# Gating an attention output before it is normalised, with one denominator product for two heads

## The chip, the cores and the metric

The kernel runs on one core of a Trainium2 chip. The metric is the device time of one execution in microseconds (us), as the median of several runs. Beside it stands a profile of one execution: which engine did what and when, what each instruction waited for, and the clock that TensorE (PE) was granted. The other engines are VectorE (DVE), ScalarE (ACT), GpSimd (POOL) and SyncE (SP), which here only issues DMAs.

## The reference

One inference step of a layer with three branches that read the same normalised input: dilated softmax attention (12 heads of 64 channels), a spatial gating unit and a gated linear recurrence. Every branch is gated by silu of its own projection, and one output projection joins them. There are 1024 prompt tokens and 8 single-token samples. What matters here is the prompt's attention. Each head evaluates three patterns of window and stride over the same keys, and combines them by their softmax denominators:

```python
PATTERNS = ((128, 1), (512, 4), (2048, 16))
...
    s = jnp.einsum('brnqhe,brnkhe->brnhqk', qb, kb, preferred_element_type=F32)
    s = jnp.where(valid[:, None], s, -jnp.inf)
    p, lse = _softmax_stats(s)
    o = jnp.einsum('brnhqk,brnkhe->brnqhe', p, vb.astype(F32))
...
    w = jax.nn.softmax(jnp.stack(lses), axis=0)
    return jnp.sum(w[..., None] * jnp.stack(outs), axis=0)
...
y = jnp.concatenate([o_a.reshape(B, L, C_A) * jax.nn.silu(z_a.astype(F32)), ...], axis=-1)
return x + jnp.einsum('bln,nd->bld', y, w_out)
```

Combined like this, the three patterns are one softmax in which each key is counted as often as patterns hold it. So for each head and query there is one sum of weighted values and one denominator: their quotient, times silu of the gate's projection, is what goes on to the output projection.

## The kernel before, in words

The attention (`attention`, line 514) goes through six pairs of heads, p = 0 to 5, two pairs to a step `sp`. For each pair `qk_proj` (287) projects queries and keys, and `qk_layout` (389) turns them so that channels lie on the partitions. For each step `v_proj` (333) projects the values of four heads, and `az_proj` (378) the gates: `Z` holds one tile `z` per pair, already silu of the projection, with the pair's two heads on partitions 0 to 63 and 64 to 127 and the tokens along the free dimension. Weights and inputs are split into a high and a low part (float32r), so that one product in full precision takes three passes of TensorE.

`attn_head` (423) does one head. First come, block by block, the products `s` of queries and keys, of which only the row maximum is kept (line 436, VectorE); the maxima go, as one more row, into the query operand. Then the head's queries are done in two halves `qc` of 512. A half goes through groups of products `st` (lines 470, 471); for each there is an exponential (473, ScalarE), a mask that also counts (476 to 485, VectorE), a cast to the high part `phi` (487, ScalarE) and the low part `plo` (488, VectorE). Lines 491 to 493 sum the weighted values in the PSUM tile `pv`: rows 0 to 63 are channels, and row 64, for which the value operand holds ones, is the denominator. In the second half one group (`parts is None`) takes every fourth key and query, so its operands are read in steps of four.

At the end of a half, before the change: ScalarE copies `pv` to SBUF as `yo` (498), and turns row 64 into its reciprocal by Ln and Exp (499, 500). TensorE spreads this one row over 64 partitions by a product with a column of ones, into `pb` (502). VectorE multiplies `yo` by `pb` into `rd`, writing the queries back in their natural order (503), and `z` by `rd` (505). After both heads SyncE stores `z` to DRAM (512), from where the output projection, the program's last stage, reads it.

The order of the work is not that of the text. The text gives each instruction its priority, and a scheduler (`TileContext` with a simulated timeline) builds each engine's queue from it, filling gaps with later work that is ready. Each engine then runs its queue strictly in order. Projections of the next pairs, and near the end those of the recurrence (`pi`, `pc`, `pcz`), so fill TensorE's gaps in the attention. What can run ahead is limited by buffers: PSUM has four tiles "st" (shared by `s`, `st` and `pb`), two for projections, one for transposes and one `pv`; SBUF has 16 large tiles (among them `z`, the projected queries and keys and the eight layout tiles of a pair) and two tiles "s2b" (`yo` and `rd`; later the recurrence's `kT` and others).

After the attention come the recurrence (`hgrn`, 744), with the samples' attention, the gating unit (`sgu`, 775) and the output projection (`out_proj`, 945). In the recurrence line 710 has a product `pn` of ones (128x128) with a tile of 512 columns.

`masks` (279) holds two masks in bf16; `cmask` has eight blocks of 128 columns, of which the last two are zero and are not read.

Of the kernel before, what the change touches and what calls it, by code (L numbers as in the profile page):

```python
# [8 lines left out]
F32 = mybir.dt.float32  # L9
# [3 lines left out]
AF = mybir.ActivationFunctionType  # L13
ALU = mybir.AluOpType
# [14 lines left out]
E = 64  # L29
# [62 lines left out]
def hybrid_step(tc, ins, outs, parts=("A", "D", "B", "C", "O"), dbg=None):  # L92
    nc = tc.nc
# [5 lines left out]
    def mm(out, lhsT, rhs, start, stop):  # L99
        nc.tensor.matmul(out, lhsT=lhsT, rhs=rhs, start=start, stop=stop)  # L100

    with tc.tile_pool(name="const", bufs=1) as cp, tc.tile_pool(name="sb", bufs=1) as sb, \
# [14 lines left out]
        def s2b(nm, dt=F32, shape=(P, 512)):  # L117
            return sb.tile(list(shape), dt, tag="s2b", name=nm, bufs=N_S2B)
# [7 lines left out]
        def psum(tag, nm, bufs, n=512):  # L126
            return pm.tile([P, n], F32, tag=tag, name=nm, bufs=bufs)
# [16 lines left out]
        def p_big(nm):  # L144
            return psum("st", nm, 4)
# [23 lines left out]
        ones = cp.tile([P, P], F32, name="ones")  # L169
# [36 lines left out]
        for t in (0, NT, *range(1, NT)):  # L206
            n = P if t < NT else NS
# [6 lines left out]
            if t == NT:  # L214
                nc.vector.tensor_tensor_reduce(out=xn[:n, :], in0=xt[:n, :], in1=xt[:n, :], op0=ALU.mult, op1=ALU.add,
                                               scale=1.0, scalar=0.0, accum_out=ss[:n, 0:1])
# [61 lines left out]
        new_k, new_v = (outs[n][0, 0].rearrange("s h e -> s (h e)") for n in ("o_kp", "o_vp"))  # L278
        masks = sb.tile([P, 2, NT, P], BF16, tag="mask", name="masks", bufs=1)
        cmask, nmask = (masks[:, i].rearrange("p a b -> p (a b)") for i in range(2))  # L280
        tc.keep_in_program_order(nc.gpsimd.dma_start(masks[:, 0], ins["cmask"]))
        tc.keep_in_program_order(nc.gpsimd.dma_start(masks[:, 1], ins["nmask"]))
        qkg = cp.tile([P, 2, 6], F32, name="qkg")
        tc.keep_in_program_order(nc.scalar.dma_start(qkg[:, 0, :], ins["q_norm_g"][0].rearrange("(a p) -> p a", p=P)))
# [138 lines left out]
        def attn_head(p, h, tiles, V, F, z):  # L423
# [3 lines left out]
            for qc in range(2):  # L427
                M = small(f"M{p}_{h}_{qc}", 12, tag="M")
                for b in range(4 * qc, 4 * qc + 4):
                    n = (b + 1) * P  # L430
# [16 lines left out]
            for qc in range(2):  # L447
                pv = p_pv(f"pv{p}_{h}_{qc}")
                pv4 = pv.rearrange("p (b r i) -> p b r i", b=4, r=4)
                groups = GROUPS[qc]  # L450
                for gi, parts in enumerate(groups):
# [4 lines left out]
                    if parts is None:  # L456
                        for r in range(4):
                            q4 = [x[:, 512:S].rearrange("p (b r i) -> p b r i", b=4, r=4)[:, :, r, :] for x in (QQ, Q1)]
                            prods.append((slice(r * P, (r + 1) * P), slice(r, 512, 4), q4, fh[:, r], fl[:, r],
                                          lambda m, r=r: pv4[0:m, :, r, :]))  # L460
# [17 lines left out]
                    elif parts[-1][0] == 3:  # L478
                        for c, m in ((0, P), (2 * P, 2 * P)):
                            n = 2 * P - c // 2  # L480
# [8 lines left out]
                    for i, (cols, _, _, v, l, out) in enumerate(prods):  # L489
# [3 lines left out]
                        mm(out(E + 1), v1, plo[:, cols], False, gi == len(groups) - 1 and i == len(prods) - 1)  # L493
                r = slice(h * E, (h + 1) * E)
                cs = slice(qc * 512, qc * 512 + 512)
                yo, rd = (s2b(f"{n}{p}_{h}_{qc}") for n in ("yo", "rd"))
                dr = yo[E:E + 1, :]
                nc.scalar.copy(yo[0:E, :], pv[0:E, :])
                nc.scalar.activation(dr, pv[E:E + 1, :], AF.Ln)  # L499
                nc.scalar.activation(dr, dr, AF.Exp, scale=-1.0)  # L500
                pb = p_big(f"pb{p}_{h}_{qc}")
                mm(pb[0:E, :], ones[E:E + 1, 0:E], dr, True, True)
                nc.vector.tensor_tensor(rd[r, :].rearrange("p (b i r) -> p b r i", b=4, r=4),
                                        *(x[0:E, :].rearrange("p (b r i) -> p b r i", b=4, r=4) for x in (yo, pb)), ALU.mult)
                nc.vector.tensor_tensor(z[r, cs], z[r, cs], rd[r, :], ALU.mult)

        def attn_core(p, nats, V, z, tiles=None):
            tiles = tiles or qk_layout(p, nats)
            F = v_far(p)
            for h in range(2):  # L510
                attn_head(p, h, tiles[h], V, F, z)
            nc.sync.dma_start(y_d[p * P:(p + 1) * P, :], z[:, :S])

        def attention():
            for sp in range(3):
                n0 = qk_proj(2 * sp, blk_first if sp == 0 else None)
                tiles = qk_layout(2 * sp, n0)
                V = v_proj(sp)
                Z = az_proj(sp)
                attn_core(2 * sp, n0, V[0], Z[0], tiles)  # L520
                n1 = qk_proj(2 * sp + 1)
                attn_core(2 * sp + 1, n1, V[1], Z[1])


        U32, U16 = mybir.dt.uint32, mybir.dt.uint16
# [504 lines left out]
        if "A" in parts:  # L1030
            attention()
# [30 lines left out]
```

## Time and profile before

| | us |
|---|---|
| median of 3 runs | 1364.37 (1363.49 to 1366.2) |
| the profiled execution | 1367.91 |
| its span, first to last instruction | 1366.1 |
| mean TensorE clock granted in it | 0.951 of full speed |

Reading it: a row of grouped instructions has line, engine, operation, output<-inputs, shapes and count, then the busy time and the mean of one in ns, then the idle time of the engine just before them and what ended it. The rows on one tile give the shortest, median and longest duration in ns instead. All matrix products have line 100 (a helper), so they are told apart by the names of their tiles. A row of a timeline has the start, the duration, and in brackets the idle time before and what ended it. A row of waits has who waited for whom, us in total, how often, and the longest. A row of windows has the stretch, its length, the busy time of each engine in it, and after these TensorE's clock, the busy share of the DMA engines and GB/s. A plain f32 product counts as two instructions, one for each pass; TensorE's matmuls overlap, so the step from one start to the next, not the duration, is what each takes.

### The profile page before, as it was taken

Reading aid. Unit: us, or ns where it says so; the run is one execution under the profiler, and the core shown is the slowest. Engines: PE = TensorE matmul, PEld = TensorE weight load, DVE = VectorE, ACT = ScalarE, POOL = GpSimd, SP = SyncE. Lnnn points to the kernel's source line nnn. Section 1 sums busy time; section 2 is a strip of 40 time slices with the busy share of each in tenths; the row PEclk is TensorE's granted clock in tenths of the full one; section 3 lists DMA queues with packets and bytes.
Section 4 is the critical chain, followed back from the end, with each engine's and each line's share of the span. In section 5 each row is a group of like instructions: output and inputs, shape, how many; then the busy total and the mean of one; then the engine's idle time right before and its main releaser. Section 6 shows DMA issues by size and latency. Waiting matters only on the chain. (4 is left out here: it accounts for less than half of the span.)

```text
span 1366.1 us, 27783 instructions
## 1 busy us (share of the span) xinstructions
PE 1277.9 (94%) x10634; PEld 1160.8 (85%) x10634; DVE 914.3 (67%) x2439; ACT 661.0 (48%) x1510; POOL 292.6 (21%) x267
## 2 busy tenths in 40 slices
PE   4799999999889999999999998998899999999999
PEld 3699798779779797898888888987788899899998
DVE  5835775565774656668888988888887623654653
ACT  4435454454443554456654744545544423544543
POOL 2531210131121212112202020211111135311221
PEclk9899899889999799999999999999999999999999
DMA  6241122220221212202433243434253313612210
GB/s 220 42 141 36 47 66 70 59 68 18 58 84 58 76 36 77 65 29 67 119 97 109 90 121 115 111 97 134 61 156 96 92 32 108 207 51 81 74 46 31
DMA packets 165044, 114.23 MB, mean 84 GB/s; under 512 B 13944, under 2 KB 158864, under 8 KB 164912
## 3 DMA queue, kind: packets, MB, share of 16 engines
q1 hardware_dynamic: 157520, 110.28, 27.3%
q10 hardware_dynamic: 6816, 1.54, 0.5%
q8 instruction: 83, 1.36, 0.4%
q0 software_dynamic: 576, 0.64, 0.3%
q14 instruction: 49, 0.40, 0.1%
HBM read 84.60 MB, written 22.09 MB: 78 GB/s over the span
## 5 line engine op out<-in xcount | busy, mean ns | idle before, releaser
L100 PE MATMUL pqk<-wh_qk,h 128*128 128x256 f32 x768 | 159.6, 299 | 5.2 <-ACT h L233 2.8
L100 PE MATMUL pc<-h,wh_cqf 128*128 128x344 f32 x576 | 144.1, 332 | 4.5 <-DVE cz L152 4.5
L100 PE MATMUL po<-woh,yl 128*128 128x256 f32 x512 | 145.0, 284 | 1.9 <-POOL yl L1011 1.9
L100 PE MATMUL po<-woh,yh 128*128 128x256 f32 x512 | 145.7, 285 | 0.0
L100 PE MATMUL po<-wol,yh 128*128 128x256 f32 x512 | 144.4, 282 | 0.0
L100 PEld LDWEIGHTS pqk<-wh_qk,h 128*128 128x128 f32 x768 | 131.5, 204 | 9.8 <-ACT h L233 3.0
L100 PE MATMUL pqk<-wl_qk,h 128*128 128x256 f32 x384 | 114.0, 297 | 0.0
L100 PEld LDWEIGHTS pc<-h,wh_cqf 128*128 128x128 f32 x576 | 102.1, 194 | 7.1 <-DVE cz L152 5.0
L100 PEld LDWEIGHTS po<-woh,yh 128*128 128x128 f32 x512 | 97.1, 190 | 5.6 <-ACT yh L1010 3.9
L100 PEld LDWEIGHTS po<-woh,yl 128*128 128x128 f32 x512 | 97.2, 190 | 4.1 <-POOL yl L1011 2.4
L100 PEld LDWEIGHTS po<-wol,yh 128*128 128x128 f32 x512 | 97.3, 190 | 0.0
L100 PE MATMUL pc<-h,wl_cqf 128*128 128x344 f32 x288 | 94.9, 332 | 2.5 <-POOL wl_cqf L193 2.2
L436 DVE CUSTOM_DVE_ANT_0 s<-s,masks 128x512 f32<-128x512 f32 (+2 forms) x144 | 77.7, 584 | 13.8 <-PE s L100 13.3
L100 PE MATMUL pi<-wh_ci,h 128*128 128x256 f32 x384 | 77.6, 297 | 4.8 <-DVE dsc L925 1.9
L100 PE MATMUL pv<-wh_v,h 128*128 128x256 f32 x384 | 79.1, 297 | 1.9 <-DVE ss L165 1.6
L473 ACT ACTIVATE st<-st 128x512 f32<-128x512 f32 (+2 forms) x84 | 44.2, 536 | 72.9 <-PE st L100 70.2
L100 PEld LDWEIGHTS pqk<-wl_qk,h 128*128 128x128 f32 x384 | 78.1, 204 | 0.5
L100 PE MATMUL pcz<-h,wh_cz 128*128 128x344 f32 x288 | 71.5, 326 | 0.3 <-DVE q L152 0.3
L100 PE MATMUL paz<-h,wh_az 128*128 128x344 f32 x288 | 71.1, 329 | 0.0
L100 PEld LDWEIGHTS pi<-wh_ci,h 128*128 128x128 f32 x384 | 64.2, 201 | 6.9 <-issue 2.9
L1011 DVE TENSOR_TENSOR yl<-yb,yh 128x512 fp32r<-128x512 f32 x44 | 30.4, 692 | 58.0 <-ACT yh L1010 58.0
L100 PEld LDWEIGHTS pv<-wh_v,h 128*128 128x128 f32 x384 | 65.7, 204 | 3.0 <-ACT yo L499 1.8
(376 smaller groups left out, 3665.1 us busy)
## 6 DMA issues: line engine op xcount, KB each, us to landing
wro<-in_w_out_dram SPq DMA_DIRECT2D x32, 256.0 KB
wr_qk<-in_w_in_dram SPq DMA_DIRECT2D x48, 128.0 KB
wr_cqf<-in_w_in_dram SPq DMA_DIRECT2D x48, 128.0 KB
dk<-in_cache_k_dram SPq DMA_DIRECT2D x24, 192.0 KB
dv<-in_cache_v_dram SPq DMA_DIRECT2D x24, 192.0 KB
xt<-in_x_prompt_dram SPq DMA_DIRECT2D x8, 512.0 KB
xr<-in_x_prompt_dram SPq DMA_DIRECT2D x32, 128.0 KB
out_o_yp_dram<-xr SPq DMA_DIRECT2D x32, 128.0 KB
```

What stands on the lines that cost most here:

```text
L100: nc.tensor.matmul(out, lhsT=lhsT, rhs=rhs, start=start, stop=stop)
L436: nc.vector.tensor_tensor_reduce(out=ps[:, :w], in0=ps[:, :w], in1=nmask[:, S - n + c:S - n + c + w], op0=ALU.add, op1=ALU.max, scale=1.0, ...
L473: nc.scalar.activation(st[:, :o], st[:, :o], AF.Exp)
L1011: (nc.gpsimd if piece == 0 else nc.vector).tensor_tensor(yl[:, sl, :], y, yh[:, sl, :].bitcast(F32), ALU.subtract)
```

## The change

The half no longer normalises. Row 64 of `pv` is copied into a row of a tile `den[qc]` (row 64 for the first head, row 96 for the second; the rest is zero), and `z` is multiplied by the channels of `pv` straight from PSUM, which also puts the queries in order. A new `normalise` does the rest, once for a pair and half: one product with a 128x128 tile `sel`, which holds ones at (64, 0 to 63) and (96, 64 to 127), puts both heads' denominators on all 128 partitions; Ln and Exp run on these in PSUM, and one multiplication of `z` by them ends it. It is called after the next pair's `qk_proj`, for the last pair at the end. `sel` lies in the two blocks of `cmask` that are not read, and the mask's load leaves these out; the two `den` are the two tiles "s2b". The store of `z` moves into `normalise`.

```diff
+        sel = masks[:, 0, 6:8].rearrange("p a b -> p (a b)").bitcast(F32)
+        tc.keep_in_program_order(nc.gpsimd.dma_start(masks[:, 0, 0:6], ins["cmask"][:, 0:6]))
-        tc.keep_in_program_order(nc.gpsimd.dma_start(masks[:, 0], ins["cmask"]))
...
-                yo, rd = (s2b(f"{n}{p}_{h}_{qc}") for n in ("yo", "rd"))
-                dr = yo[E:E + 1, :]
-                nc.scalar.copy(yo[0:E, :], pv[0:E, :])
-                nc.scalar.activation(dr, pv[E:E + 1, :], AF.Ln)
-                nc.scalar.activation(dr, dr, AF.Exp, scale=-1.0)
-                pb = p_big(f"pb{p}_{h}_{qc}")
-                mm(pb[0:E, :], ones[E:E + 1, 0:E], dr, True, True)
-                nc.vector.tensor_tensor(rd[r, :].rearrange("p (b i r) -> p b r i", b=4, r=4),
-                                        *(x[0:E, :].rearrange("p (b r i) -> p b r i", b=4, r=4) for x in (yo, pb)), ALU.mult)
-                nc.vector.tensor_tensor(z[r, cs], z[r, cs], rd[r, :], ALU.mult)
+                nc.scalar.copy(den[qc][E + 32 * h:E + 32 * h + 1, :], pv[E:E + 1, :])
+                zv = z[r, cs].rearrange("p (b i r) -> p b r i", b=4, r=4)
+                nc.vector.tensor_tensor(zv, zv, pv4[0:E], ALU.mult)
...
+        def normalise(p, z):
+            for qc in range(2):
+                cs = slice(qc * 512, qc * 512 + 512)
+                pb = p_big(f"pb{p}_{qc}")
+                mm(pb, sel, den[qc], True, True)
+                nc.scalar.activation(pb, pb, AF.Ln)
+                nc.scalar.activation(pb, pb, AF.Exp, scale=-1.0)
+                zv = z[:, cs].rearrange("p (b i r) -> p b r i", b=4, r=4)
+                nc.vector.tensor_tensor(zv, zv, pb.rearrange("p (b r i) -> p b r i", b=4, r=4), ALU.mult)
             nc.sync.dma_start(y_d[p * P:(p + 1) * P, :], z[:, :S])
+        den = [s2b(f"den{i}") for i in range(2)]
+        for t in (sel, *den):
+            nc.gpsimd.memset(t, 0.0)
+        for h in range(2):
+            nc.gpsimd.memset(sel[E + 32 * h:E + 32 * h + 1, h * E:(h + 1) * E], 1.0)
...
         def attention():
+            done = None
             for sp in range(3):
                 n0 = qk_proj(2 * sp, blk_first if sp == 0 else None)
+                if done:
+                    normalise(*done)
                 tiles = qk_layout(2 * sp, n0)
                 V = v_proj(sp)
                 Z = az_proj(sp)
-                attn_core(2 * sp, n0, V[0], Z[0], tiles)
+                done = attn_core(2 * sp, n0, V[0], Z[0], tiles)
                 n1 = qk_proj(2 * sp + 1)
-                attn_core(2 * sp + 1, n1, V[1], Z[1])
+                normalise(*done)
+                done = attn_core(2 * sp + 1, n1, V[1], Z[1])
+            normalise(*done)
```

More of the change, by code (lines that the diff above doesn't have):

```diff
@@ L511, in attn_core @@
                 attn_head(p, h, tiles[h], V, F, z)
-            nc.sync.dma_start(y_d[p * P:(p + 1) * P, :], z[:, :S])
+            return p, z
+        def normalise(p, z):
[7 more added lines that the diff above has]
+                nc.vector.tensor_tensor(zv, zv, pb.rearrange("p (b r i) -> p b r i", b=4, r=4), ALU.mult)
+            nc.sync.dma_start(y_d[p * P:(p + 1) * P, :], z[:, :S])
+        den = [s2b(f"den{i}") for i in range(2)]
[3 more added lines that the diff above has]
+            nc.gpsimd.memset(sel[E + 32 * h:E + 32 * h + 1, h * E:(h + 1) * E], 1.0)
         def attention():
+            done = None
             for sp in range(3):
                 n0 = qk_proj(2 * sp, blk_first if sp == 0 else None)
+                if done:
+                    normalise(*done)
                 tiles = qk_layout(2 * sp, n0)
```

## The prediction

> **What bounds the kernel now.** I read the page first, then the attention stage in the table of windows, the instructions of tile `yo`, TensorE's waits, the timeline around `pb`, and the clock in windows of 3.41 us.
>
> ```profile
> span 1366.1 us, 27783 instructions
> ...
> PE 1277.9 (94%) x10634; PEld 1160.8 (85%) x10634; DVE 914.3 (67%) x2439; ACT 661.0 (48%) x1510; POOL 292.6 (21%) x267
> ```
> ```profile
> 118.00:690.00 572.00, 542.06 (x3631) 478.56 (x3630) 382.80 (x941) 287.88 (x614) 108.65 (x109) 0.92 0.22 63
> ```
>
> TensorE (PE) bounds the program: 1277.9 of 1366.1 us busy. In the attention stage (118 to 690 us; columns: length, busy PE, PEld, DVE, ACT, POOL, granted clock, DMA) it is idle for 572 - 542.06 = 29.9 us, and a mean clock of 0.92 takes 572 × 0.08 = 46 us more. Three things pay here: less work on PE, fewer waits of PE, less time at the low clock.
>
> The change touches the end of each of the 24 half heads:
>
> ```profile
> L100 PE MATMUL pb<-yo,ones x48: 587/638/1111, 133.0 to 668.4; 1*64 1x512 f32 x48
> L498 ACT COPY yo<-pv x24: 566/580/583, 128.5 to 662.5; 64x512 f32<-64x512 f32 x24
> L499 ACT ACTIVATE yo<-pv x24: 588/590/592, 129.1 to 663.0; 1x512 f32<-1x512 f32 x24
> L500 ACT ACTIVATE yo<-yo x24: 608/627/629, 130.3 to 664.3; 1x512 f32<-1x512 f32 x24
> ```
> ```profile
> PE pb L100 <- ACT yo L500: 12.5, 5, 3.2
> ```
> ```profile
> 132.98 1.07 PE L100 MATMUL pb<-yo,ones 1*64 1x512 f32 x2
> 133.98 0.51 PE L100 MATMUL st<-QQ,KK 128*128 128x512 f32 x1
> ```
> ```profile
> 260.48 0.28 PE L100 MATMUL pv<-pl,vh 128*65 128x256 f32 x1
> 263.25 1.96 PE L100 MATMUL pb<-yo,ones 1*64 1x512 f32 x2 [2.49 <-ACT yo L500]
> 265.14 0.80 PE L100 MATMUL st<-QQ,KK 128*128 128x512 f32 x1
> ```
>
> After the last `pv` ScalarE copies and takes Ln and Exp (0.58 + 0.59 + 0.63 us); then PE spreads the one row, two passes in 1.00 us (132.98 to 133.98), and only behind it come the next `st`. Projections mostly fill the time; five times nothing was left, and PE stood still for 12.5 us in all, as at 260.76.
>
> The low clock comes in whole windows of 3.41 us on a fixed grid. First the seven windows that hold a `pb` of a head's first half and are full of work; then what follows each:
>
> ```profile
> 133.27:136.68 3.41, 3.41 (x15) 2.65 (x14) 2.36 (x3) 0.79 (x2) 0.61 (x1) 1.00 0.13 38
> ...
> sum 23.88, PE 23.88 PEld 17.77 DVE 15.28 ACT 9.30 POOL 3.64; mean PE 3.41 PEld 2.54 DVE 2.18 ACT 1.33 POOL 0.52
> ```
> ```profile
> 136.68:140.09 3.41, 3.41 (x17) 3.40 (x17) 2.59 (x4) 1.94 (x4) 0.00 (x0) 0.50 0.00 0
> ...
> sum 40.97, PE 40.36 PEld 37.86 DVE 31.10 ACT 23.25 POOL 1.27; mean PE 5.77 PEld 5.41 DVE 4.44 ACT 3.32 POOL 0.18
> ```
>
> PE had no idle time in any of the seven, and yet the clock then fell to 0.50 for one to three windows: 40.36 busy us at half speed, 20.2 us lost. After the five waits it fell too:
>
> ```profile
> 262.99:276.65 13.66, 12.87 (x52) 9.82 (x53) 9.01 (x14) 5.74 (x11) 0.00 (x0) 0.50 0.19 47
> ...
> sum 34.14, PE 33.10 PEld 26.59 DVE 27.55 ACT 17.50 POOL 11.71; mean PE 6.62 PEld 5.32 DVE 5.51 ACT 3.50 POOL 2.34
> ```
>
> That is 33.10 / 2 = 16.5 us. Behind every first-half `pb` stands the same block of `st`, whose loads are slow. Is it the block or the product that brings the clock down? Two windows tell:
>
> ```profile
> 176.70 1.07 PE L100 MATMUL pb<-yo,ones 1*64 1x512 f32 x2
> ```
> ```profile
> 177.65:181.06 3.41, 3.41 (x19) 3.32 (x19) 3.25 (x6) 1.99 (x6) 0.00 (x0) 1.00 0.31 71
> 181.06:184.48 3.42, 3.42 (x31) 3.42 (x30) 3.39 (x10) 2.96 (x6) 0.00 (x0) 1.00 0.02 5
> 904.69:908.11 3.42, 1.97 (x19) 1.07 (x21) 3.34 (x10) 0.86 (x2) 0.00 (x0) 1.00 0.25 79
> 908.11:911.52 3.41, 3.36 (x114) 3.04 (x114) 2.60 (x8) 3.35 (x8) 0.00 (x0) 1.00 0.28 82
> ```
> ```profile
> 906.54 1.12 PE L100 MATMUL pn<-csq,ones 128*128 128x512 f32 x2
> ```
>
> At 176.70 the grid puts `pb` into the window before (only 0.04 us falls into this one), the whole block into 177.65 to 181.06, and the clock stays at 1.00. So the block alone does not do it; a product with one row of weights seems to count as almost no work. The product `pn`, of the new product's shape (128 rows, 128 columns, 512 wide, f32), does count: its window is busy for only 1.97 us, over half of that with `pn`, and the clock holds.
>
> **The Trainium skill** ("TensorE: Matmul & The Clock Gate", Part 1) says the same of the window (free-running, about 3.4 us, half clock after an idle one), and the trace agrees. But its rule is about idle gaps: by that rule the seven full windows owe nothing to `pb`. That is rival B.
>
> **The change part by part.** The sum is made against the profiled execution: 1367.91 us, 1.8 outside its span, and 3.5 above the median of 1364.37.
>
> Work of PE. 24 products of one row go, 12 with 128 rows come. `pn` takes 1.12 us where `pb` takes 1.07, so each slot stays 1.0 to 1.05: -24.0 + 12.2 = **-11.8**.
>
> Waits of PE. The chain copy, Ln, Exp before a product becomes one copy of a row (0.58; the rows of L498 and L499 bound it at 0.57 and 0.59), and the product moves to the pair's end. Late next at 260.76 is the `st` block, which at 265.14 waits for nothing once `pb` is out. Of 12.5 I take two thirds, **-8**: the last third stays where the new product comes straight after the pair's last copy, because the projections that it stands behind were already used up as filling. Bounds: 0 and -12.5.
>
> Clock. Bounds: 0, and -20.2 - 16.5 = -36.7. I take three quarters of the seven full windows, **-15**, and nothing of the rest, since idle time from other causes can bring those down as well.
>
> ScalarE loses 24 × 1.80 = 43 us and gains 24 × 0.58 + 24 × 0.58 = 28 (Ln and Exp of 128x512, the row of L473 below). With 288 of 572 busy, this is worth nothing by itself.
>
> ```profile
> L193 POOL TENSOR_TENSOR wl_qk<-wr_qk,wh_qk 128x512 fp32r<-128x512 f32 x24 | 32.7, 1387 | 66.3 <-ACT wh_qk L192 64.9 <-DMA wr_qk<-in_w_in_dram 1.4
> ```
>
> POOL's five memsets (two of 128x512, the others smaller) run at the start, while POOL waits for ScalarE's casts (64.9 us of its idle time over the run end with one); uncovered they are shorter than two of L193, 2.8 us once. SyncE's six stores of `z` move behind the next pair's loads and `ko` stores; the loads queued behind a store then wait for the last multiplication, as they now wait for L505; what the stores write is read only in the last stage. `z` keeps its one of 16 buffers through the next projections; the next pair's eight layout tiles need the eight of this pair, which come free sooner. Were a layout to wait for `z` after all, that is the pair's end below once more, 6 × 2 = 12 us.
>
> VectorE:
>
> ```profile
> L503 DVE TENSOR_TENSOR rd<-yo,pb 64x512 f32<-64x512 f32 x24 | 25.8, 1077 | 48.2 <-PE pb L100 48.0
> L505 DVE TENSOR_TENSOR az<-az,rd 64x512 f32<-64x512 f32 x24 | 18.8, 785 | 0.6
> L488 DVE TENSOR_TENSOR pl<-st,ph 128x512 fp32r<-128x512 f32 x60 | 40.2, 684 | 2.5 <-ACT ph L487 1.7
> L414 DVE SCALAR_TENSOR_TENSOR Q<-tr,qkg,QQ 64x128 fp32r<-64x128 f32 x80 | 22.8, 347 | 15.2 <-ACT QQ L411 15.2
> L481 DVE SCALAR_TENSOR_TENSOR st<-st,masks 128x128 f32<-128x128 f32 x12 | 3.5, 292 | 0.1
> L485 DVE SCALAR_TENSOR_TENSOR st<-st,masks 128x512 f32<-128x512 f32 x48 | 32.7, 693 | 8.5 <-ACT st L473 8.1
> ```
> ```profile
> L473 ACT ACTIVATE st<-st 128x512 f32<-128x512 f32 x60 | 34.6, 582 | 62.6 <-PE st L100 60.1 <-DVE cz L152 2.0
> L487 ACT CAST ph<-st 128x512 fp32r<-128x512 f32 x60 | 34.0, 586 | 3.5 <-DVE st L485 3.1 <-DVE st L476 0.2
> ```
> ```profile
> ACT QQ L411 <- DVE Q L414: 11.3, 6, 4.1
> ```
>
> L503 writes every fourth element and takes 1.077; the contiguous L488 takes 0.684. The new multiplications both read and write `z` in that step. Bounds for one: 1.08 (reading costs nothing more) and 1.08 + 0.39 = 1.47 (it costs as much as writing). L414, which reads in this step, takes 0.055 more than L481 on 128 elements, 0.22 on 512: 1.30, my value. In all 36 × 1.30 = 46.8 for 24 × 1.862 = 44.7.
>
> The pair's end: behind its last `pv` VectorE now does three of these for one L503 and L505, 3.90 - 1.86 = 2.04 more, just where the next pair's `s` need it: 6 × 2.04 = 12.2, of which I put half on the path, **+6**.
>
> The handover of `pv`, of which there is one buffer: L411 waits for L414 in another half of the same PSUM tile, so I expect the multiplication to wait for the copy: 0.58 + 1.30 = 1.88 until `pv` is free, for 1.17 now, 0.71 later. Behind that wait stand the next half's masks on VectorE and its `pv` on PE. Cover: that `pv` needs exp, mask, cast and difference first (0.58 + 0.69 + 0.59 + 0.68 = 2.54). Without cover 24 × 0.71 = 17; I take a sixth, **+3**.
>
> Sum: -11.8 - 8 - 15 + 6 + 3 = -25.8: 1342.1 by the profiled execution, **1338.6** by the median. PE is busy for 94% of the whole span, so what follows the stage is bound by it too, and the gain should reach the end.
>
> **The rivals.**
>
> A, all the low windows go, and all the waits: -11.8 - 12.5 - 36.7 + 9 = -52, 1312. For it: after 262.99 the low clock lasted four windows, the block running at half speed. Against: of the 46 us, 0.5 × (40.97 + 34.14) = 37.6 stand behind a `pb` or its wait; 8 are low clock of another cause, so other gaps bring it on as well. Chance 0.12.
>
> B, the low clock is not the product's doing: -11.8 - 8 + 9 = -10.8, 1353.6. For it: the block is in all seven windows. Against: 177.65. Chance 0.14.
>
> C, "behind the projections" holds in name only, and reading in steps costs its full 0.39: then 3 × 1.47 - 1.86 = 2.55 at each pair's end, 15.3 in all, and 0.88 at each handover, half of it open, 10.6; with the waits gone and the clock as it is -11.8 - 12.5 + 25.9 = +1.6, 1366, no change. For it: L503's price for writing. Against: L414's. Chance 0.10. The Trainium skill ("SBUF — State Buffer", section "Door 1: The DMA port swizzle", the note on 16-byte cachelines) lets every access that goes to a new line pay, reads too; by that rule C's price is right; no run so far shows a multiplication that reads SBUF in this step.
>
> D, slower: VectorE holds the single `pv`. It is busy for 67% of the stage, so the multiplication may stand behind one more operation (0.69): 0.58 + 0.69 + 1.47 = 2.74 for 1.17, 1.6 us a half. If PE has nothing to put there, 24 × 1.6 = 38, and without a gain in clock -11.8 - 12.5 + 38 = +14: 1378. It decides from (11.8 + 12.5) / 24 = 1.0 us of idle PE a half on. For it: five times PE had nothing else. Against: the `st` block is now free to fill the gap. Chance 0.14.
>
> **How the numbers follow.** The forecast keeps 0.50 (its own range 1326 to 1352). About 0.2%, 2.7 us, is what a measurement can tell from no change. Faster: the forecast, A and B, 0.76; same: C, 0.10; slower: D, 0.14. The range 1310 to 1366 takes in all but D and some tails.
>
> **What would show it.** Right: 24 passes of the new product with 128 rows; PE's waits for it under 4 us; no window of 3.41 us that is full of work followed by clock 0.50; the stage's clock above 0.94; multiplications near 1.30. Wrong: `pv` waiting for VectorE's multiplication in PE's list, the clock still at 0.92, `s` waiting at each pair's start.

## The result, and the profile after

The changed kernel takes 1289.34 us (median of four runs, 1287.74 to 1294.63), the kernel before beside it 1363.93: a ratio of 0.9451, 95% interval 0.9429 to 0.9472. That is 74.6 us less, where 25.8 were forecast; the range, 1310 to 1366, ends above it. The profiled execution took 1287.74 us.

First the head of the page and, from the table of windows, the attention stage (before, this was 118 to 690 us; now it ends at about 585):

```profile
span 1286.0 us, 27698 instructions
...
PE 1215.2 (94%) x10610; PEld 1129.3 (88%) x10610; DVE 916.5 (71%) x2427; ACT 644.2 (50%) x1486; POOL 285.5 (22%) x272
```
```profile
118.00:585.00 467.00, 454.21 (x3330) 420.75 (x3329) 349.49 (x863) 253.28 (x551) 98.02 (x104) 0.98 0.25 71
```

TensorE is still the bound, but its clock in the stage is 0.98 instead of 0.92, and VectorE and ScalarE are busier in a shorter stage. The stage gave more than the whole program kept. The last store of `z` in SyncE's timeline, before and after:

```profile
672.49 0.35 SPq L512 DMA_DIRECT2D y_scr<-az  x1
```
```profile
572.99 0.34 SPq L517 DMA_DIRECT2D y_scr<-az  x1
```

99.5 us earlier, while the span is 80.1 shorter: the other 19.4 us are projections of the recurrence that had filled gaps in the attention and now run behind it (253 products `pc` start ahead of that store before, 144 after).

The groups of the new half's and pair's end, and TensorE's list of waits in the stage, from its top:

```profile
L499 DVE TENSOR_TENSOR az<-az,pv 64x512 f32<-64x512 f32 x24 | 26.1, 1088 | 13.5 <-ACT den L497 13.2
L497 ACT COPY den<-pv 1x512 f32<-1x512 f32 x24 | 13.9, 578 | 23.7 <-PE pv L100 23.5
L516 DVE TENSOR_TENSOR az<-az,pb 128x512 f32<-128x512 f32 x12 | 13.1, 1088 | 4.8 <-ACT pb L514 4.8
L100 PE MATMUL pb<-den,masks 128*128 128x512 f32 x24 | 12.3, 596 | 0.0
```
```profile
PE s L100 <- DMA QQ<-QQ: 6.9, 3, 2.4
PE pc L100 <- DVE cz L152: 2.7, 1, 2.7
PE pqk L100 <- DVE nat L304: 1.1, 2, 0.7
PE pv L100 <- DVE pl L489: 0.9, 1, 0.9
```

No wait for `pb` is left, and none of `pv` for the multiplication. The multiplications take 1.09 us. What low clock is left in the stage up to its last 3 us (four windows) stands behind idle time, as here:

```profile
179.70:183.10 3.40, 1.04 (x9) 0.84 (x7) 2.08 (x8) 1.22 (x2) 0.00 (x0) 1.00 0.17 39
183.10:189.90 6.80, 6.15 (x28) 5.43 (x27) 6.57 (x24) 2.26 (x5) 0.74 (x1) 0.50 0.33 77
```

Every profiled execution can be split in the same way, from the first lines of its page and its mean clock: idle time of PE is span less PE's busy time; what the low clock took is span × (1 - clock); the rest is PE's work at full clock. Before: idle 88.2, low clock 66.9, rest 1210.9. After: 70.8, 29.6, 1185.6. So of 80.1 us, **37.3 are clock, 25.3 work, 17.4 idle time**. (The clock has three digits, so its part is good to 1 us or so. Idle time inside half clock counts whole as idle time and by half as low clock, so the rest is too small by that half; it is 7 to 13 us in all kernels but the two that are named below.)

### The profile page after: what moved, and what is told of

The parts are those of the page before. It is cut to its first block, busy times and chain, and to the rows that moved or that the text cites. A ratio compares the mean times of both kernels' runs of the same rounds, so it can differ in the third digit from the quotient of the medians.

```text
span 1286.0 us, 27698 instructions
## 1 busy us (share of the span) xinstructions
PE 1215.2 (94%) x10610; PEld 1129.3 (88%) x10610; DVE 916.5 (71%) x2427; ACT 644.2 (50%) x1486; POOL 285.5 (22%) x272
## 4 chain that ended last, share of the span: by engine, by line
PE 75%; DVE 15%; DMA 4%; issue 3%; ACT 2%; SPq 0%; POOL 0%; ACTq 0%; DVEq 0%; POOLq 0%
PE po L100 15%; PE pqk L100 10%; PE pv L100 9%; PE paz L100 5%; PE pi L100 5%; PE st L100 4%; PE pbu L100 4%; PE pc L100 4%; PE pbz L100 4%; PE pbv L100 3%; PE pcz L100 2%; PE s L100 2%; DMA dk<-in_cache_k_dram 2%; DVE T L628 2%; DVE T L630 1%
## 5 line engine op out<-in xcount | busy, mean ns | idle before, releaser
L100 PEld LDWEIGHTS pqk<-wh_qk,h 128*128 128x128 f32 x768 | 127.8, 197 | 12.3 <-ACT h L233 4.3
L100 PE MATMUL pv<-wh_v,h 128*128 128x256 f32 x384 | 75.3, 287 | 0.3 <-DVE ss L164 0.3
L100 PE MATMUL pcz<-h,wh_cz 128*128 128x344 f32 x288 | 72.2, 330 | 2.3 <-DVE q L152 2.3
L100 PEld LDWEIGHTS pv<-wh_v,h 128*128 128x128 f32 x384 | 61.8, 193 | 1.9 <-issue 1.2
L1027 ACT CAST yh<-yb 128x512 fp32r<-128x512 f32 x64 | 39.6, 620 | 43.4 <-PE po L100 43.4
```

The source lines that it names most:

```text
L1027: nc.scalar.copy(yh[:, sl, :], y)
```

## The experiments

The table has all kernels, with their medians; a ratio is to runs of the kernel before that were made beside that kernel (medians of 1363.9 to 1366.6). The split is that of one profiled execution, which can lie some us off the median: 1297.7 for "after, at once", 1354.0 for "at the half's end", 1310.9 for "after + 12 of 1 x 64". The last column counts what the prediction's clock term rested on: windows of 3.41 us on the clock's grid that hold a half's product (or the extra product of four kernels), are full of work, and yet are followed by half clock.

| kernel | median us | ratio to before [95%] | clock | low clock | idle | rest | full, then half |
|---|---|---|---|---|---|---|---|
| before | 1363.9 | 1 | 0.951 | 66.9 | 88.2 | 1210.9 | 7 |
| after | 1289.3 | 0.945 [0.943, 0.947] | 0.977 | 29.6 | 70.8 | 1185.6 | 0 |
| before, 65 rows | 1361.9 | 0.998 [0.996, 1.000] | 0.955 | 61.2 | 85.9 | 1211.9 | 6 |
| before, other PSUM tile | 1360.7 | 0.998 [0.996, 0.999] | 0.955 | 61.2 | 111.2 | 1187.9 | 0 |
| both of these | 1370.4 | 1.005 [1.003, 1.007] | 0.951 | 67.2 | 118.9 | 1184.6 | 0 |
| gate from PSUM alone | 1360.4 | 0.998 [0.996, 1.000] | 0.953 | 63.8 | 91.3 | 1202.1 | 5 |
| after, at once | 1290.6 | 0.946 [0.943, 0.949] | 0.970 | 38.9 | 72.2 | 1184.8 | 0 |
| after, one-row products | 1301.1 | 0.953 [0.951, 0.955] | 0.975 | 32.5 | 70.6 | 1198.8 | 0 |
| at the head's end | 1313.1 | 0.962 [0.960, 0.963] | 0.974 | 34.1 | 72.2 | 1206.6 | 0 |
| at the half's end | 1358.7 | 0.995 [0.992, 0.998] | 0.960 | 54.1 | 89.6 | 1208.4 | 5 |
| ahead of the far group | 1338.7 | 0.982 [0.979, 0.985] | 0.960 | 53.4 | 76.9 | 1205.6 | 6 |
| behind the far group | 1341.8 | 0.984 [0.981, 0.986] | 0.966 | 45.6 | 83.1 | 1212.4 | 1 |
| a quarter of the first half | 1336.0 | 0.980 [0.977, 0.982] | 0.963 | 49.3 | 84.2 | 1199.4 | 2 |
| after + 12 of 1 x 64 | 1316.8 | 0.965 [0.961, 0.969] | 0.965 | 45.8 | 66.0 | 1197.1 | 8 |
| after + 12 of 1 x 128 | 1317.0 | 0.964 [0.962, 0.967] | 0.966 | 44.7 | 72.3 | 1198.3 | 7 |
| after + 12 of 128 x 128 | 1291.9 | 0.947 [0.945, 0.949] | 0.976 | 31.0 | 68.2 | 1193.7 | 0 |
| after + 12 of 1 x 64, unstepped | 1298.8 | 0.950 [0.946, 0.953] | 0.968 | 41.6 | 70.1 | 1187.5 | 4 |
| after, unstepped | 1278.5 | 0.937 [0.936, 0.938] | 0.977 | 29.3 | 69.8 | 1176.8 | 0 |
| before, unstepped | 1340.6 | 0.983 [0.981, 0.985] | 0.964 | 48.3 | 91.1 | 1202.2 | 1 |
| before, 65 rows and 128 columns | 1344.9 | 0.985 [0.982, 0.987] | 0.968 | 42.9 | 89.4 | 1208.5 | 1 |

### Rows, and another place in PSUM

More rows of weights in the old product (all zeros but one), its place unchanged:

```diff
-                mm(pb[0:E, :], ones[E:E + 1, 0:E], dr, True, True)
+                mm(pb[0:E, :], sel[0:E + 1, 0:E], yo[0:E + 1, :], True, True)
```

> The kernel before, with one thing changed: the product that spreads the reciprocal takes 65 rows (the copied channels too, with weights of zero for them) instead of one. Work, waits and almost the whole order of the work stay. Clock theory (a product with one row counts as idle time for the clock): none of the seven full windows of 3.41 us is followed by clock 0.50 any more, about 20 us less, 1344, and the stage's mean clock rises from 0.92 to about 0.95; TensorE's 12.5 us of waits for the product stay. Path theory (the next scores stand behind the product in TensorE's queue, and its chain on ScalarE makes TensorE wait): no change, 1364. Luck theory (the gain comes from a re-made order of the work): no change, 1364.

Six full windows are still followed by half clock, and the time is the same within its interval; the clock theory had none of them, and 1344. So the number of rows alone is not it. Next, `pb` taken from the transposes' PSUM tile, so that the next `st` need not stand behind it in the shared four buffers, with one row and with 65:

```diff
-                pb = p_big(f"pb{p}_{h}_{qc}")
+                pb = p_tr(f"pb{p}_{h}_{qc}")
```

> The kernel before, with one thing changed: the one-row product writes the PSUM tile of the transposes instead of one of the four that it shares with the scores, so that the next scores need not stand behind it. Path theory: TensorE's 12.5 us of waits for the product go, and with them part of the 16.5 us of low clock behind them; 1364 - 12 to - 29, 1335 to 1352. Clock theory: the one-row products are all still there, and the seven full windows lose at most those in which product and slow scores now fall apart; the clock stays below 0.95. If neither moves, 1364, the shared tiles were not what ordered them.

> The kernel before with both edits: 65 rows in the product, and its own PSUM tile. If clock and path are two causes that add up: 1364 - 20 - 20 = about 1324, stage clock 0.96 or more, no waits for the product. If the two are one (the low clock comes from the waits and the order), no better than the better of the two single edits.

The full windows go, and the waits for `pb` too, but there is one such tile, and the next pair's transposes now wait for it. TensorE's waits, top line, of the kernel with one row:

```profile
PE tr L399 <- DVE KK L414: 33.0, 11, 3.2
```

Idle time rises by 23 us and brings low clock of its own, so that it is 1360.7 and not the path theory's 1335 to 1352; with 65 rows it is 1370.4, no better. In these two kernels 41 and 40 us of idle time lie inside half clock, so their low rest is for the most part not less work. The two runs mix two changes, and say only that one wait was exchanged for another.

### The gate alone

The kernel before with only the gating moved: `z` times `pv` from PSUM, but each half still takes Ln, Exp and its one-row product at once.

> One part of the change alone: the gate times the unnormalised result from PSUM, but each half of each head still takes Ln, Exp, its own one-row product and a second multiplication at once (24 products, none shared, none moved). Clock theory: one-row products ahead of the slow scores as before, so the low windows stay. Path theory: the chain before the product is as long as before, the waits stay. Both: 1364, or 10 to 15 slower for the second multiplication in steps (24 x 1.08 us for 24 x 0.69). If it comes near the changed kernel's 1289, the gating itself, which frees the result's PSUM tile without ScalarE's copy, was the gain.

1360.4: of the change's first half, for itself, hardly anything comes. What pays is in the rest.

### The place of the product

Four kernels go from the change back towards that, step by step. The first calls `normalise` directly behind a pair's second head:

```diff
-                done = attn_core(2 * sp, n0, V[0], Z[0], tiles)
+                normalise(*attn_core(2 * sp, n0, V[0], Z[0], tiles))
```

> The changed kernel, with each pair's normalisation written directly behind its second head and not behind the next pair's projections. Theory P (it is the half's end that is relieved; where behind the pair's end the product stands does not matter): 1289, within 4 us of the changed kernel. Rival B (the projections ahead of it hide the copy, the product and the rest of the chain): six pairs' ends with PE or the next pair waiting some 3 us each, 1307.

1290.6, the same. "Behind the projections" holds in name only: the scheduler puts the product at the pair's end in both. The second has the one-row products again, two a half, at that place:

```diff
-                mm(pb, sel, den[qc], True, True)
+                for h in range(2):
+                    d = E + 32 * h
+                    mm(pb[h * E:(h + 1) * E, :], sel[d:d + 1, h * E:(h + 1) * E], den[qc][d:d + 1, :], True, True)
```

> The changed kernel, where each product of 128 rows and 128 columns is two products of one row and 64 columns again (24 in all), at the same place behind the pair's end; Ln, Exp and the second multiplication stay shared. Theory P (place): only the work comes back, 12 times (2 x 1.00 - 0.86) = +13.7 us, 1303, granted clock about 0.975 as in the changed kernel. Rival M (the narrow one-row products themselves bring the low clock, wherever they stand): the clock falls towards 0.955 over the attention, +13.7 and another 20 to 37 us, 1323 to 1340.

1301.1, with the clock at 0.975: the rest grows by 13.2 us, the work of the products, and little else moves (low clock 2.9 us more). Only seven of the twelve pairs of products stood one behind the other. In the other five the two heads' products, which read other rows and write other partitions, ran side by side, four passes in the time of two:

```profile
164.56 1.07 PE L100 MATMUL pb<-den,masks 1*64 1x512 f32 x4
165.56 0.27 PE L100 MATMUL pv<-ph,fh 128*65 128x128 f32 x1
```

The third shares nothing between heads: at each head's end its two halves take one-row products, and Ln, Exp and the second multiplication on 64 partitions. The fourth does the same at each half's end:

```diff
             for h in range(2):
                 attn_head(p, h, tiles[h], V, F, z)
+                normalise(p, h, z, range(2))
```
```diff
                 nc.vector.tensor_tensor(zv, zv, pv4[0:E], ALU.mult)
+                normalise(p, h, z, [qc])
```

> The changed kernel, where nothing is shared between heads: at each head's end two one-row products of 64 columns from the copied denominators, with Ln, Exp and the second multiplication on 64 partitions for each (24 of each in all). Theory P (place: out of the way of the two halves inside a head): +13.7 us of work as in the kernel with one-row products at the pair's end, and about half of what the place gave, since the second half's product of each first head again stands inside the pair: 1303 to 1330. Rival S (what pays is the sharing: half as many Ln, Exp, products and multiplications): near the kernel that only gates from PSUM, 1355 to 1362.

> As the kernel with the products at each head's end, but each half's product stands directly at that half's end, taken from the copied denominators, with Ln and Exp behind it on 64 partitions rather than ahead of it on one row. Theory P (the place at the half's end, ahead of the next half's scores in the shared buffers, is what cost): 1350 to 1362, clock 0.95 to 0.955, as the kernel that only gates from PSUM. Rival K (the chain of Ln and Exp ahead of the product was the cost; behind the product it holds up nobody on PE): 1303 to 1315, clock 0.975.

1313.1 and 1358.7. These two differ only in where the product of a head's first half is issued, and that is worth 45.6 us. The profiled executions are 39.0 apart: 20.0 of low clock, 17.4 idle, the rest 1.8. That Ln and Exp now stand behind the product and not ahead of it (rival K) changes next to nothing: 1358.7 against 1360.4 for the gate alone. In the timeline of the kernel with products at the head's end, the second half's `st` follows the last `pv` without a step between:

```profile
129.45 0.28 PE L100 MATMUL pv<-pl,vh 128*65 128x256 f32 x1
129.57 0.46 PE L100 MATMUL st<-Q,K 65*128 65x512 f32 x2
```

With products at the half's end it stands behind `pb`, and `pb` behind the copy; projections fill the time from 129.5 on:

```profile
132.14 1.07 PE L100 MATMUL pb<-den,masks 1*64 1x512 f32 x2
133.13 0.50 PE L100 MATMUL st<-QQ,KK 128*128 128x512 f32 x1
```

So the second half of the head starts some 3.5 us later. Where projections are lacking, PE waits (its list of waits in the stage, first line):

```profile
PE pb L100 <- ACT den L497: 7.1, 5, 2.5
```

### The place inside the second half

The first half's product between the scores of the second half's first group and the far group (`parts is None`, the eight stepped products), or behind the latter (there `gi == 2`):

```diff
                 for gi, parts in enumerate(groups):
+                    if qc and gi == 1:
+                        normalise(p, h, z, [0])
```

> As the kernel with one-row products at each head's end (1313.1), but the first half's product stands inside the second half, between the scores of its first group and the eight stepped score products of its far group. By then its denominators are copied, so it waits for nothing, yet it lies in one window with the eight. Theory Q (what cost at the half's end was that the second half's scores stood on PE behind a product that waits for the copy): 1313 to 1318. Theory R (a window of 3.41 us that holds the product and the eight stepped ones is followed by half clock, as the prediction had it): five to nine full windows followed by 0.50, each 1.7 us lost, 1322 to 1329.

> The same with the first half's product behind the eight stepped score products, ahead of the second half's last group. Theories Q and R alike: 1313 to 1318, no full window followed by 0.50. Together with the kernel that has it ahead of the eight, the difference of the two is R's price alone.

1338.7 and 1341.8, above the bounds of both theories, by 10 and 24 at the least. The claim that the product waits for nothing there was wrong. TensorE's lists of waits, first of the one ahead of the far group, then of the one behind it:

```profile
PE pb L100 <- ACT den L499: 6.6, 5, 1.9
```
```profile
PE pb L100 <- ACT den L499: 4.1, 5, 0.9
```

The full windows behave as theory R has it: six are followed by half clock with the product ahead of the eight, one with it behind them, and the low clock takes 7.8 us less. But the rest is 6.8 larger in the second, for a reason that I have not found, and the times do not part.

A quarter of the first half's product at its old place, the half's end (three of four blocks of these halves stay without their denominators):

```diff
+                w = 512 if qc else P
-                mm(pb, sel[d:d + 1, r], den[qc][d:d + 1, :], True, True)
+                mm(pb[:, 0:w], sel[d:d + 1, r], den[qc][d:d + 1, 0:w], True, True)
```

> As the kernel with each half's product at that half's end (1358.7), but the first half's product, its Ln, Exp and second multiplication cover only 128 of the 512 queries (the other three blocks of the first half stay without their denominators). Its place and its wait for the copy stay, the product takes about a quarter of the 1.07 us. Theory Q: only the work goes, 12 x 0.75 = 9 us, 1348 to 1352. Theory R: the product no longer fills a third of the window, the full windows followed by 0.50 go too, 1335 to 1342.

1336.0, in R's bounds; full windows followed by half clock are two instead of five. Low clock, idle time and the rest each fell by 5 to 9 us, so it is no proof by itself.

### An extra product, in three sizes

These three are the clearest. Into the changed kernel goes, at each first half's end, an extra product ready as soon as the half's last product is, so that nobody waits; its result is not used. The three have the same order of instructions on every engine, and differ in this line alone:

```diff
+                    dm = p_big(f"dm{p}_{h}")
+                    for i in range(2):
+                        mm(dm[0:E, i * 256:(i + 1) * 256], ones[0:1, 0:E], plo[0:1, 0:256].bitcast(F32), True, True)
```
```diff
-                        mm(dm[0:E, i * 256:(i + 1) * 256], ones[0:1, 0:E], plo[0:1, 0:256].bitcast(F32), True, True)
+                        mm(dm[:, i * 256:(i + 1) * 256], ones, plo[:, 0:256].bitcast(F32), True, True)
```
```diff
-                        mm(dm[0:E, i * 256:(i + 1) * 256], ones[0:1, 0:E], plo[0:1, 0:256].bitcast(F32), True, True)
+                        mm(dm[:, i * 256:(i + 1) * 256], ones[0:1, :], plo[0:1, 0:256].bitcast(F32), True, True)
```

> The changed kernel with an extra product at each first half's end (12 in all, each two of one row, 64 columns and 256 wide on the half's last weights; its result is not used), in the shared score buffers, directly ahead of the second half's scores, ready as soon as the half's last product is. Theory Q (the wait for the copy is the cost): only work, 12 x 1.0, 1301 to 1304, clock 0.975. Theory R (product and eight stepped ones in one window): five to nine low windows more, 1310 to 1317. Theory P in its bare form (anything at that place costs what the product cost there): 1289 + 45 = 1334.

> The kernel with the 12 extra products, with nothing but their size changed: 128 rows and 128 columns in place of one row and 64 columns, the same order on every engine. Theory A (half clock follows a window in which a narrow product and the stepped ones use little of the array; a full product would not count): the full windows followed by 0.50 go, 1316.8 less some 8 x 1.7 = 14, 1303 within 4. Theory L (any product of that length ahead of the eight stepped ones does it): 1310 to 1317.

> The kernel with the 12 extra products, now of one row and 128 columns (128 x 128 gave 1291.9, one row and 64 columns 1316.8; the same order on every engine in all three). If the columns are what counts: 1291 to 1295, no full window followed by 0.50 in the attention. If the rows are (or both must be there): 1310 to 1320.

Twelve products of one row and 64 columns cost 27.5 us, of one row and 128 columns 27.7, of 128 rows and 128 columns 2.6. The last is better than theory A had it, which took only the eight full windows off: 1291.9 against 1303 within 4. Low clock differs by 14.8 us between the profiled executions of 1 x 64 and 128 x 128, which are 16.0 apart where the medians are 24.9. The granted clock of the four runs of each was 0.956 to 0.966 with 1 x 64, 0.960 to 0.966 with 1 x 128, and 0.976 to 0.984 with 128 x 128. For each size one product in its timeline, and the window that holds it and the eight stepped ones, with the window behind (the last three columns are the clock, the DMA share and GB/s). One row, 64 columns:

```profile
240.33 1.07 PE L100 MATMUL dm<-pl,ones 1*64 1x256 f32 x4
241.33 0.50 PE L100 MATMUL st<-QQ,KK 128*128 128x512 f32 x1
```
```profile
240.29:243.70 3.41, 3.41 (x16) 2.78 (x16) 2.54 (x3) 1.64 (x3) 0.00 (x0) 1.00 0.35 79
243.70:247.11 3.41, 3.41 (x17) 3.41 (x17) 2.09 (x3) 2.13 (x4) 0.00 (x0) 0.50 0.00 0
```

One row, 128 columns:

```profile
239.09:242.50 3.41, 3.41 (x17) 2.98 (x17) 2.53 (x3) 1.49 (x4) 0.00 (x0) 1.00 0.33 75
242.50:245.91 3.41, 3.41 (x18) 3.41 (x18) 2.25 (x4) 2.39 (x5) 0.00 (x0) 0.50 0.00 0
```

128 rows, 128 columns:

```profile
289.52 1.03 PE L100 MATMUL dm<-pl,ones 128*128 128x256 f32 x4
290.20 0.58 PE L100 MATMUL st<-QQ,KK 128*128 128x512 f32 x1
```
```profile
289.00:292.41 3.41, 3.41 (x19) 3.22 (x17) 2.84 (x6) 1.16 (x2) 0.74 (x1) 1.00 0.09 29
292.41:295.83 3.42, 3.42 (x29) 3.42 (x29) 2.46 (x5) 3.00 (x6) 0.00 (x0) 1.00 0.03 10
```

All three windows are full by the records; only behind the big product does the clock hold. With 1 x 64 half clock follows at nine of the twelve places, at eight of them behind a full window. In the three where the clock held (products at 128.99, 459.95 and 572.52) the product starts 1.15 to 1.35 us into its window, so that less than 0.7 us of the eight lies in it; in the eight that were followed by half clock it is 1.0 us or more. With 128 x 128 no place is followed by half clock, though in six of the twelve the product and at least 1.2 us of the eight share a window, and four of these are full.

The big product also keeps TensorE for less time: the eight start 1.33 us behind it, and 1.57 behind one of 1 x 64. But it is not the time. Two windows hold the eight whole. In the first only the last 0.2 us of a product of 1 x 64 (403.30 to 404.30) stand ahead of them, in the second a whole product of 128 x 128 (from 159.30 on). Half clock follows the first:

```profile
404.12:407.53 3.41, 3.41 (x19) 3.19 (x18) 2.26 (x4) 1.44 (x4) 0.00 (x0) 1.00 0.17 38
407.53:410.95 3.42, 3.42 (x19) 3.42 (x18) 3.22 (x7) 3.37 (x7) 0.00 (x0) 0.50 0.22 77
```
```profile
159.29:162.71 3.42, 3.42 (x19) 3.27 (x18) 1.81 (x2) 1.34 (x3) 1.86 (x2) 1.00 0.12 38
162.71:166.12 3.41, 3.41 (x34) 2.37 (x33) 2.95 (x6) 3.34 (x7) 0.64 (x1) 1.00 0.01 4
```

### The eight stepped products

The far group's keys taken as four runs of neighbouring columns (other keys than the reference's, as many products, the same order on every engine), in the kernel before, the one with 12 products of 1 x 64, and the change:

```diff
-                            prods.append((slice(r * P, (r + 1) * P), slice(r, 512, 4), q4, fh[:, r], fl[:, r],
+                            prods.append((slice(r * P, (r + 1) * P), slice(r * P, (r + 1) * P), q4, fh[:, r], fl[:, r],
```

> The kernel before, with the keys of the far group taken as four runs of 128 neighbouring columns instead of every fourth column (other keys than the reference's; the same products, the same order on every engine). Theory R (the eight stepped products are the other half of the low windows): 12 x 8 x about 0.12 us = 11 us of work go, and the full windows followed by 0.50 behind a first half's product go as well (some 8 x 1.7 = 14): 1336 to 1345. Rival N (the step does not make them slow): 1361 to 1366.

> The kernel with the 12 extra one-row products, with the far group's keys unstepped in the same way. Theory R: 1316.8 - 11 - 14, 1290 to 1296, no full window followed by 0.50 in the attention. Rival N: 1310 to 1317. If the step costs work but has no part in the clock: 1303 to 1307.

> The changed kernel with the far group's keys unstepped in the same way: it has no full window followed by 0.50 in the attention to lose, so only the 11 us of work go: 1276 to 1282. It is the ground against which the kernel with extra products and unstepped keys is read: 12 x 1.0 us between the two by theory R. Rival N: 1287 to 1291.

From one start to the next in the timelines, first of the change, then of the change with unstepped keys:

```profile
127.70 0.40 PE L100 MATMUL st<-QQ,KK 128*128 128x128 f32 x1
127.94 0.40 PE L100 MATMUL st<-Q,K 65*128 65x128 f32 x1
128.17 0.40 PE L100 MATMUL st<-QQ,KK 128*128 128x128 f32 x1
```
```profile
128.10 0.28 PE L100 MATMUL st<-QQ,KK 128*128 128x128 f32 x1
128.21 0.28 PE L100 MATMUL st<-Q,K 65*128 65x128 f32 x1
128.32 0.28 PE L100 MATMUL st<-QQ,KK 128*128 128x128 f32 x1
```

0.235 against 0.11 us: the step doubles them. The change gains 10.8 us without it, as expected. The kernel before gains 23.4, and six of its seven full windows go. The kernel with 12 narrow products gains 18.0, which lies between theory R and work alone, and keeps four of eight. So the slow eight have a part in it, and the narrow product next to unstepped ones can still be enough.

### A wider product in the kernel before

> The kernel before, with each half's product of 65 rows and 128 columns in place of one row and 64 columns, at its old place at the half's end, of which 64 columns are used. Its waits stay. If 65 rows and 128 columns use enough of the array: the full windows followed by 0.50 behind a first half's product go, some 8 x 1.7 = 14 us, 1347 to 1353 (65 rows and 64 columns gave 1361.95 and kept them). If not: 1359 to 1366.

The kernel with 65 rows has only its columns widened, from 64 to 128 (`sel[0:E + 1, :]` into all of `pb`, of which 64 partitions are used): 1361.95 becomes 1344.9, somewhat below the 1347 to 1353 that were expected, and six full windows followed by half clock become one. First a window of the narrow form with what follows, then of the wide one:

```profile
640.19:643.60 3.41, 3.41 (x15) 2.57 (x14) 2.52 (x4) 2.94 (x8) 3.41 (x3) 1.00 0.53 153
643.60:647.01 3.41, 3.41 (x25) 2.54 (x24) 3.41 (x6) 2.27 (x6) 0.62 (x2) 0.51 0.57 164
```
```profile
217.63:221.04 3.41, 3.41 (x17) 2.89 (x17) 2.24 (x3) 0.69 (x2) 0.00 (x0) 1.00 0.45 154
221.04:224.45 3.41, 3.41 (x30) 3.41 (x29) 3.03 (x7) 3.03 (x6) 0.00 (x0) 1.00 0.00 0
```

1 x 64, 1 x 128 and 65 x 64 bring the half clock, 65 x 128 (but for one place) and 128 x 128 do not, the sizes with 65 rows tried in the kernel before, those with 128 rows or 128 columns alone in the changed one: neither rows nor columns do it alone. In the order of rows times columns the five fall apart cleanly, between 4160 and 8320; that it is this product that counts is the simplest reading, and no run here excludes another.

## Why the prediction was wrong

The direction and the mechanism of the clock were right; the sum was 49 us short by the medians. By the profiled executions it was 54 short: 22 in the clock, 14 in the work, 9 in the waits, and 9 that it had added. Its terms, against these executions:

**Work, -11.8.** The new product's slot was taken as 1.0 to 1.05 us. It is 0.86: the next product starts 0.46 us behind it, and then takes 0.52 where its neighbours take 0.12. So the step from start to start alone does not tell what a product costs.

```profile
169.20 1.02 PE L100 MATMUL pb<-den,masks 128*128 128x512 f32 x2
169.66 0.68 PE L100 MATMUL pqk<-wl_qk,h 128*128 128x256 f32 x1
170.18 0.40 PE L100 MATMUL pqk<-wh_qk,h 128*128 128x256 f32 x2
170.42 0.27 PE L400 MATMUL tr<-ident,nat 128*128 128x128 f32 x1
```

24 × 1.00 less 12 × 0.86 is 13.7. But the rest fell by 25.3: some 12 us of PE's time at full clock lie in other instructions. A part is in `s`, the products for the row maximum: of those with 512 columns at full clock, 22 of 69 took over 0.3 us to the next start before the change (recorded idle time left out), and 3 of 71 after it. They are not in the one place: the rest climbs by 13.2, 7.8 and 1.8 us on the way back from the change over one-row products and the head's end to the half's end. The prediction had no term for it, and its cause stays open.

**Waits, -8.** Idle time fell by 17.4. "The last third stays where the new product comes straight after the pair's last copy" did not come true: there the product finds something else on PE, or the next pair's work, and the list has no wait for it. The step between the products at the head's end and at the half's end shows as much, 17.4, for the first half's product alone.

**Clock, -15: the step that failed.** The prediction took "three quarters of the seven full windows, -15, and nothing of the rest, since idle time from other causes can bring those down as well". Measured are 37.3, as much as its own outer bound of 36.7. All seven full windows went, and most of the half clock behind idle time went too: with the wait its idle time, and with that what followed it. Behind the discount stood only that some 8 of the stage's 46 us were low clock of another cause; for leaving out the half clock behind the five waits, or a quarter of the full windows, there was no row. That the narrow product, not the eight stepped ones, tips a full window is confirmed by the extra products; "a product with one row of weights seems to count as almost no work" was too narrow, since 65 rows with 64 columns count as little. Rival B (the clock is not the product's doing, 0.14) falls by the same three runs.

The Trainium skill ("TensorE: Matmul & The Clock Gate", Part 1) has the half clock come after an idle window; here it followed windows whose records show 3.41 of 3.41 us busy, so what is counted is not the busy time that the profile shows. Nor were the windows ahead of the other half clocks in the stage wholly idle: in the kernel before there are nine, and TensorE was busy for 0.46 to 2.78 us of them. The trace agrees with the page on the window's length and fixed grid alone.

**The pair's end, +6, and the handover, +3.** Both came out at nothing. The multiplications take 1.09 us, not 1.30, together 26.1 + 13.1 = 39.2 us against 25.8 + 18.8 = 44.6 of the two that they replace. `pv` is indeed freed late, as foreseen: VectorE stood idle for 13.2 us ahead of L499, waiting for the copy of row 64. But PE's `pv` did not wait for it: its list has 0.9 us in the stage, for the low part of the weights. Rival D had to find 1.0 us a half; its cover, the `st` block, was there.

Rival C's first half was right, that "behind the projections" is a name only, and it cost nothing. Its second half, the price of reading in steps, was wrong. The Trainium skill ("SBUF — State Buffer", section "Door 1: The DMA port swizzle") lets each access to a new 16-byte line pay; a multiplication that reads and writes SBUF in steps of four f32 took 1.088, one that only wrote in them 1.077, so here reading adds nothing to see.

Of the rivals A was nearest: all low windows and all waits, at 1312. Without the +9 and with 17.4 for the waits its sum would be -11.8 - 17.4 - 36.7 = -65.9, and the 12 us of the unexplained rest bring it to what was measured. It had 0.12.

What the change does can be read off the ladder of the place: 1289.3 as it is; 1301.1 with twice as many, narrow products (their work); 1313.1 with nothing shared between heads; 1358.7 with each first half's product back at that half's end (waits and clock); 1363.9 before. The greatest step, 45.6 of 74.6 us, is one product a head taken out of the way of the next half's scores. A part of it can be had otherwise: making the old product wider at its old place gives 1344.9, 17 less than the narrow one with as many rows.

## What to carry over

A small product that must wait for another engine belongs where nothing of the same chain stands behind it on TensorE; its price is not its microsecond but the wait, and the half clock behind the wait. Where such a product has to stand next to slow, short products, give it many rows and columns even if most of the weights are zeros (65 by 128 were enough here but for one place). And where a term of a sum has an outer bound from rows, a discount on it needs a row too.

## What the runs showed of the hardware

A product of 128 rows and 128 columns lets the next one start earlier than one of one row: in the rows above the next `st` starts 0.68 us behind it instead of 1.00. A part of this is lost again, since that `st` then takes 0.42 instead of 0.34. Twelve of them added 8.1 us to the rest, where twelve narrow ones added 11.5 (64 columns) and 12.7 (128 columns).

Weights of zeros were no hindrance: of the weights of 65 x 128 all rows but one are zeros, and behind full windows the clock held at all places but one.

Two one-row products that read other rows and write other partitions ran side by side five times, four passes of 512 columns in 1.00 us.

Loading 128 columns of weights with a step of four f32 and running 128 columns through them took 0.235 us from start to start, 0.11 without the step.
